# A decoder layer on one core: attention softmax in fewer VectorE instructions, three more chunks by seven products, six hand-overs reordered

## The chip, the core and the metric

The kernel runs on one core of a Trainium2 chip. The core has a matrix engine (TensorE, PE in the profile; PEld is its weight load), a vector engine (VectorE, DVE), a scalar engine that evaluates functions (ScalarE, ACT), a general one (GpSimd, POOL) and a queue engine that starts transfers (SyncE, SP). They run beside each other and wait for each other by semaphores. The metric is the device time of one execution in microseconds; less is better.

## The reference

One layer, 256 tokens of width 2048 in float32, batch 1. Two half-step SwiGLU blocks stand around a mixer of two branches:

```python
h = layer_norm(DN_ALPHA * h + 0.5 * swiglu(h, ffn1_w_in, ffn1_w_out), ln1_g, ln1_b)
q, k, v, qi, ki, wi, rx, rg, gates = split_cols(h @ w_in)
y_attn = dsa_attention(rope(q), rope(k), v, rope(qi), rope(ki), wi * c)   # 16 heads of 128, 4 key heads
y_rnn = rglru_branch(rx, rg, conv_w, conv_b, lru_wa, lru_ba, lru_wx, lru_bx, lru_lambda)
g_attn, g_rnn = split(sigmoid(gates), 2)
merged = g_attn * (y_attn @ w_attn_branch) + g_rnn * (y_rnn @ w_rnn_branch)
h = layer_norm(DN_ALPHA * h + merged @ w_out, ln2_g, ln2_b)
h = layer_norm(DN_ALPHA * h + 0.5 * swiglu(h, ffn2_w_in, ffn2_w_out), ln3_g, ln3_b)
```

The attention is sparse: an indexer scores every key for every query, the 64 best causal keys of a query are kept, and a head's softmax goes over these alone:

```python
_, idx = lax.top_k(score, topk)                     # topk = 64
s = where(valid, (q . k[idx]) * HEAD_DIM ** -0.5, -inf)
p = softmax(s);  o = p . v[idx]
```

## The kernel before, in words

**Numbers in two halves.** Matrices are multiplied in float32 precision from two reduced-precision halves: a weight piece `raw` becomes `wh` (a rounded copy, ACT, L243) and `wl` (the rest, DVE, L244), an activation tile becomes a high and a low half in the same way (for instance L860 on ACT and L861 on DVE, L803 and L804). A product is three matmuls: high by high, high by low, low by high (L674 to L676 over feature-major weights, L688 to L691 in pairs). Weights are streamed once: SP loads pieces of 128 x 1024, five of each half are kept, so L243 and L244 run a few pieces ahead of PE, and L243 of a piece waits until PE has finished with the `wh` five pieces before.

**Chunks by seven products.** Most products go by chunks of four 128 x 512 weight tiles. A plain chunk is 24 matmuls of 512 columns in two pieces. A chunk can also be computed with Strassen's seven products in Winograd's form: 42 matmuls of 256 columns in three and a half pieces (`blockF`, forms `p1q3`, `p2`, `q5p7` and the last). Its weights are sums that DVE makes first (L206, L210, L213), its activations are sums as well (`left`, L589 to L595, the tiles `sh` and `sl`), and at the end `joined` (L1178 to L1184) puts the block together from the products. `GATE_FAST` lists, for each of the eight blocks of 512 gate columns, which of the four chunks go this way.

**Order.** PE, SP and POOL run in the order in which the code is written. DVE and ACT are ordered by a scheduler ahead of time, with some work marked as of high priority. Small work between products is written as generators in lanes: at every new weight piece each lane makes one step (`on_piece`). So a step's distance in time is the length of a piece, 12 matmuls, of 512 columns or of 256.

**The heads.** In the middle of the gate blocks 0 to 5, sixteen heads pass through the lane `head`, four at a time (`head(h)`, L1247 on). The steps: scores on PE into PSUM (L1258, L1259; 128 + 256 columns for the two query tiles); scale and mask in one DVE pass (L1262) and the row maximum by two reductions (L1267); two exponentials with row sums on ACT (L1270); reciprocal of the sums and two products on DVE (L1272, L1274); three transposes on PE (L1278); the copy out on ACT (L1281); the product with the values (L1284, L1285). Before them the indexer makes the mask `bias` on DVE: the sum over 16 index heads (L1234), eight rounds of maximum and replace (L1239, L1240), and two closing steps (L1244, L1245). Between these, DVE runs a chain of small 128 x 20 instructions for the recurrent branch's constants (L516 to L567).

**The seams.** Where a layer norm stands between two products, PE cannot go on until the first tiles of the normed activation are there. `InnerNorm` does it for the first and second norm: `half(t)` norms the first two 512-wide blocks of token half t (L871), transposes them on PE (L852), scales and shifts them on ACT (L859, or L874 for later blocks), and splits them (L860, L861). Blocks 2 and 3 come by `Lazy`, which makes block number `k // 4 + 1 + ahead` when tile k is asked for; a block costs transposes (L885), scaling (L874) and splitting (L803, L804). Meanwhile `eager` runs the first eight k steps (L674 to L676, tiles `hs`). The last norm, `OuterNorm.finish`, computes the second token half at the end: statistics, the reciprocal root on POOL (L825, a power), products on DVE (L931, L935), a part on PE by a diagonal matrix `dg` (L946, L950), and the stores. Between the mixer and its output product the merged activation `mg` is split (L803, L804) and, for seven-product chunks, summed by `left_again`.

**The start.** SP loads the activation tiles `x` and the first weight pieces in turns.

Of the kernel before, what the change touches and what calls it, by code (L numbers as in the profile page):

```python
# [106 lines left out]
GATE_FAST = ((), (), (), (3,), FAST_A, FAST_A, (), ())  # L107
# [192 lines left out]
class Lazy:  # L300


    def __init__(self, n, per, make, ahead=1):
        self.n, self.per, self.make, self.ahead = n, per, make, ahead
        self.tiles = []
        self.made = 0
        self.halves = None
# [4 lines left out]
    def __getitem__(self, k):  # L312
        while self.made < min(self.n // self.per, k // self.per + 1 + self.ahead):
            self.tiles += self.make(self.made)
            self.made += 1
        return self.tiles[k]
# [3 lines left out]
def tile_layer(ctx, tc, x_fm, x_tm, pos, f1a, f1o, wA, wki, wB, wG, lru, wab, wrb, wo, f2a, f2o,  # L320
# [136 lines left out]
    W.load_to(3, load_x_fm)  # L457
    for k2 in range(4, NK // 2):
        load_x_fm(k2)
# [109 lines left out]
    with tc.manual_schedule():  # L569
        for k2 in range(4):  # L570
            xs += split_x(k2)
            W.split_to(k2, (256, 512, PIECE, PIECE)[k2])
        for k2 in range(4, NK // 2):
            xs += split_x(k2)
# [33 lines left out]
    def left_again(x, forms, chunks):  # L608

        for k in (2 * q + r for q in chunks for r in range(2)):  # L610
            f = [T1(), T1()]
            for c in range(2):
                V.tensor_tensor(f[c], x[2 * k + c][:, 0], x[2 * k + c][:, 1], op=OP.add)
            yield
            left(f, forms, k)
            yield
# [147 lines left out]
    def blockA(x, finish=None, lag=0, ln=None):  # L764

        ps = [MM(), MM()]
        n = len(x)

        def half(t, k, w):
            tokens(ps[t], x[k], t, w, k == 0, k == n - 1)

        k = 0
        if getattr(x, "halves", None):
            eager(x, ps)
            k = 8
        lead = 2 * lag
        ranges = [(k, k + 2) for k in range(k, n, 2)]
        if finish:  # L780
            ranges = ranges[:-lag] + [(n - lead, n)]
        for k0, k1 in ranges:
            ws = []
            for k in range(k0, k1):
                ws.append(W.unit(512))
                half(0, k, ws[-1])
            if finish and k1 == n:
                finish(ps)
            for k in range(k0, k1):
                if ln and k == n - 2:  # L790
                    ln.half(0)
                half(1, k, ws[k - k0])
        return ps
# [22 lines left out]
    class Norm:  # L816
        last = False

        def chain(self, t):
# [5 lines left out]
            G.tensor_tensor(r, ve, mhalf, op=OP.pow)  # L825
# [3 lines left out]
    class InnerNorm(Norm):  # L829


        def __init__(self, gk, bk, fast, after):
            self.gk, self.bk, self.fast, self.after = gk, bk, fast, after
            self.hs = Lazy(NK, 4, self.block, 2)
# [8 lines left out]
        def emit(self, t):  # L843
# [4 lines left out]
            for nb in range(2):  # L848
# [4 lines left out]
                for j in range(4):  # L853
# [5 lines left out]
                    A.activation(f, src, AF.Identity, scale=col(self.gk, k), bias=col(self.bk, k))  # L859
# [12 lines left out]

        def out(self, k, hl, f, src):
            A.activation(f, src, AF.Identity, scale=col(self.gk, k), bias=col(self.bk, k))  # L874
            split(hl, f)
# [25 lines left out]
    class OuterNorm(Norm):  # L901
# [7 lines left out]
        def load(self):  # L909


            for v in (self.g, self.b):
# [4 lines left out]
                self.rows.append([t[:, nb * 512:(nb + 1) * 512] for nb in range(4)])  # L917

# [332 lines left out]
    def head(h):  # L1251
# [10 lines left out]
        V.scalar_tensor_tensor(s, ps[:, :3 * P], ATT_SCALE, bias, op0=OP.mult, op1=OP.add)  # L1262
# [3 lines left out]
        for t in range(2):  # L1266
            V.tensor_reduce(nm[:, t:t + 1], part[t], axis=AX, op=OP.max, negate=True)  # L1267
        yield
        for t in range(2):
            A.activation(part[t], part[t], AF.Exp, bias=nm[:, t:t + 1], accum_out=sm[:, t:t + 1])  # L1270
        yield
        V.reciprocal(sm, sm)  # L1272
        for t in range(2):
            V.tensor_scalar(part[t], part[t], sm[:, t:t + 1], None, op0=OP.mult)  # L1274
# [230 lines left out]
    bg.add("left", left_again(mg, mg_forms, MG_FORMS))  # L1505
# [105 lines left out]
```

## Time and profile before

| | us |
|---|---|
| runs, median of 3 (lowest, highest) | 2243.09 (2242.83, 2244.89) |
| the profiled execution | 2242.38 |
| its span in the trace | 2240.6 |
| PE busy in the span | 2223.4 (99%), 14582 matmuls |
| DVE busy | 2101.5 (94%), 3019 instructions |
| ACT busy | 1434.7 (64%), 2008 instructions |

The profiled execution takes 1.8 us more than its span, before the first and after the last instruction; it lies 0.7 us under the median. A row of a timeline gives start, duration, engine, line, operation, output and inputs, shapes, count, and in brackets the idle time ahead of it with what ended it. A row of the waits gives who waited for whom, the total, the count and the longest. Line numbers are those of the kernel before. Matmuls overlap in the pipeline, so PE's pace is read from the distance of two starts and not from a row's duration.

### The profile page before, as it was taken

Reading aid. Unit: us, or ns where it says so; the run is one execution under the profiler, and the core shown is the slowest. Engines: PE = TensorE matmul, PEld = TensorE weight load, DVE = VectorE, ACT = ScalarE, POOL = GpSimd, SP = SyncE. Lnnn points to the kernel's source line nnn. Section 1 sums busy time; section 2 is a strip of 40 time slices with the busy share of each in tenths; the row PEclk is TensorE's granted clock in tenths of the full one; section 3 lists DMA queues with packets and bytes.
Section 4 is the critical chain, followed back from the end, with each engine's and each line's share of the span. In section 5 each row is a group of like instructions: output and inputs, shape, how many; then the busy total and the mean of one; then the engine's idle time right before and its main releaser. Section 6 shows DMA issues by size and latency. Waiting matters only on the chain.

```text
span 2240.6 us, 38639 instructions
## 1 busy us (share of the span) xinstructions
PE 2223.4 (99%) x14582; PEld 2056.5 (92%) x14582; DVE 2101.5 (94%) x3019; ACT 1434.7 (64%) x2008; POOL 125.5 (6%) x196
## 2 busy tenths in 40 slices
PE   9999999999999999999999999999999999999998
PEld 8999999999988898899999999988899999999997
DVE  8999999999988999899868879998999999999997
ACT  7666666666657655665567786555666666666663
POOL 0000000000000000001000002100000000000001
PEclk9999999999999999999999999999999999999999
DMA  9776766666675555648566658766677666676655
GB/s 344 232 232 218 244 216 217 236 223 237 221 250 188 179 197 172 209 137 306 194 192 195 197 188 317 273 212 205 219 239 228 232 227 233 228 241 213 221 200 188
DMA packets 126187, 498.62 MB, mean 223 GB/s; under 512 B 14608, under 2 KB 17424, under 8 KB 107312
## 3 DMA queue, kind: packets, MB, share of 16 engines
q1 hardware_dynamic: 107424, 451.98, 57.5%
q0 software_dynamic: 18576, 44.17, 8.5%
q8 instruction: 114, 1.87, 0.3%
q14 instruction: 73, 0.60, 0.1%
HBM read 464.63 MB, written 10.49 MB: 212 GB/s over the span
## 4 chain that ended last, share of the span: by engine, by line
PE 94%; DVE 3%; ACT 1%; issue 1%; DMA 1%; SPq 0%; POOL 0%; POOLq 0%; DVEq 0%; ACTq 0%
PE mm L688 20%; PE mm L689 20%; PE mm L691 20%; PE bp L689 6%; PE bp L691 6%; PE bp L688 6%; PE mm L1387 3%; PE mm L1388 3%; PE mm L1389 3%; DVE wl L244 1%; PE mm L674 1%; PE mm L676 1%; PE bp L1071 1%; PE mm L675 1%; ACT f L874 0%
## 5 line engine op out<-in xcount | busy, mean ns | idle before, releaser
L243 ACT ACTIVATE wh<-raw 128x1024 fp32r<-128x1024 f32 (+1 forms) x569 | 574.3, 1028 | 299.8 <-PE mm L689 170.7
L244 DVE TENSOR_TENSOR wl<-raw,wh 128x1024 fp32r<-128x1024 f32 (+1 forms) x569 | 662.6, 1185 | 82.2 <-ACT wh L243 81.5
L243 ACT ACTIVATE wh<-rf 128x1024 fp32r<-128x1024 f32 (+1 forms) x438 | 393.9, 914 | 199.0 <-PE mm L689 105.9
L244 DVE TENSOR_TENSOR wl<-rf,wh 128x1024 fp32r<-128x1024 f32 (+1 forms) x438 | 451.9, 1045 | 7.5 <-ACT wh L243 1.5
L688 PE MATMUL mm<-wh,hs 128*128 128x512 f32 (+1 forms) x872 | 297.3, 350 | 0.0
L689 PE MATMUL mm<-wh,hs 128*128 128x512 f32 (+1 forms) x872 | 292.1, 344 | 0.0
L688 PE MATMUL mm<-wh,g 128*128 128x512 f32 x656 | 249.3, 380 | 0.0
L689 PE MATMUL mm<-wh,g 128*128 128x512 f32 x656 | 248.6, 379 | 0.0
L243 ACT ACTIVATE wh<-ws 128x1024 fp32r<-128x1024 f32 x146 | 155.1, 1063 | 121.2 <-PE mm L689 72.1
L688 PE MATMUL bp<-wh,sh 128*128 128x256 f32 x876 | 213.7, 278 | 0.0
L689 PE MATMUL bp<-wh,sl 128*128 128x256 f32 x876 | 210.7, 275 | 0.0
L691 PE MATMUL mm<-wl,hs 128*128 128x512 f32 (+1 forms) x872 | 205.1, 344 | 0.0
L206 DVE TENSOR_TENSOR ws<-rf 128x1024 f32<-128x1024 f32 x146 | 178.5, 1223 | 5.0 <-DMA rf<-wab 1.6
L244 DVE TENSOR_TENSOR wl<-ws,wh 128x1024 fp32r<-128x1024 f32 x146 | 178.5, 1222 | 3.8 <-ACT wh L243 3.5
L688 PEld LDWEIGHTS mm<-wh,hs 128*128 128x128 f32 x872 | 165.8, 190 | 15.3 <-issue 1.3
L689 PEld LDWEIGHTS mm<-wh,hs 128*128 128x128 f32 x872 | 165.9, 190 | 13.6
L1387 PE MATMUL mm<-hs,wh 128*128 128x256 f32 x640 | 176.4, 276 | 0.0
L1389 PE MATMUL mm<-hs,wl 128*128 128x256 f32 x640 | 176.0, 275 | 0.0
L1388 PE MATMUL mm<-hs,wh 128*128 128x256 f32 x640 | 176.0, 275 | 0.0
L689 PEld LDWEIGHTS bp<-wh,sl 128*128 128x128 f32 x876 | 168.1, 192 | 1.2
L688 PEld LDWEIGHTS bp<-wh,sh 128*128 128x128 f32 x876 | 168.0, 192 | 1.2
L691 PE MATMUL mm<-wl,g 128*128 128x512 f32 x656 | 168.3, 379 | 0.0
(368 smaller groups left out, 4888.0 us busy)
## 6 DMA issues: line engine op xcount, KB each, us to landing
rf<-f1a SPq DMA_DIRECT2D x57, 1024.0 KB, 6.4
rf<-f2a SPq DMA_DIRECT2D x57, 1024.0 KB, 6.2
raw<-f1o SPq DMA_DIRECT2D x88, 512.0 KB, 7.8
raw<-f2o SPq DMA_DIRECT2D x88, 512.0 KB, 7.8
raw<-wB SPq DMA_DIRECT2D x80, 512.0 KB, 4.3
raw<-f2a SPq DMA_DIRECT2D x62, 512.0 KB, 4.0
raw<-f1a SPq DMA_DIRECT2D x61, 512.0 KB, 4.0
raw<-wG SPq DMA_DIRECT2D x54, 512.0 KB, 4.0
```

Source lines behind the costliest of these rows:

```text
L206: v.tensor_tensor(t, b[:, 0:4:3], b[:, 1:2].to_broadcast([P, 2, 4, P]), op=OP.add)
L243: nc.scalar.activation(hp, src, AF.Copy)
L244: self.last = nc.vector.tensor_tensor(lp, src, hp, op=OP.subtract)
L674: T.matmul(ps, xh, w[0], start=start, stop=False)
L675: T.matmul(ps, xh, w[1], start=False, stop=False)
L676: T.matmul(ps, xl, w[0], start=False, stop=stop)
L688: T.matmul(ps, xh, w[0], start=start, stop=False)
L689: T.matmul(ps, xl, w[0], start=False, stop=False)
L691: T.matmul(ps, xh, w[1], start=False, stop=stop)
L1387: T.matmul(ps, w[0], xh, start=first, stop=False)
L1388: T.matmul(ps, w[0], xl, start=False, stop=False)
L1389: T.matmul(ps, w[1], xh, start=False, stop=last)
```

## The change

1. `GATE_FAST`: chunk 3 of blocks 1 and 2 and chunk 2 of block 3 go by seven products as well.
2. The head softmax: L1262 and L1267 become one DVE instruction per query tile, straight from PSUM, which adds the mask to the scores, multiplies by the negative scale and gives the row minimum of the result; each is followed by a short read of that minimum (`ISA` rows in the order). The exponential takes scale -1. The two products by the reciprocal (L1274) become two scaled copies on ACT.
3. `InnerNorm`: of the scalings, every second one of the second token half and every odd tile of blocks 2 and 3 are done by DVE instead of ACT; a later block is made two tiles later; after the first FFN the transposes of the first token half stand one k step (three matmuls) later.
4. `left_again` for `mg` starts four steps later and makes two steps into one.
5. The last norm's second half takes a root on ACT and a reciprocal on DVE in place of POOL's power; a dummy root is issued earlier.
6. At the start, only two x and weight pairs are loaded ahead; the rest is issued behind a one-column DVE copy of the first split tile.

```diff
-GATE_FAST = ((), (), (), (3,), FAST_A, FAST_A, (), ())
+GATE_FAST = ((), (3,), (3,), FAST_A, FAST_A, FAST_A, (), ())
...
-        while self.made < min(self.n // self.per, k // self.per + 1 + self.ahead):
+        while self.made < min(self.n // self.per, (k + self.early) // self.per + 1 + self.ahead):
...
-    W.load_to(3, load_x_fm)
-    for k2 in range(4, NK // 2):
-        load_x_fm(k2)
+    W.load_to(1, load_x_fm)
...
             xs += split_x(k2)
+            if k2 == 0:
+                V.tensor_copy(xraw[2][:, :1], xs[0][:, 1, :1])
+                W.load_to(3, load_x_fm)
+                for j in range(4, NK // 2):
+                    load_x_fm(j)
...
-    def left_again(x, forms, chunks):
+    def left_again(x, forms, chunks, lag=0):
+        for _ in range(lag):
+            yield
...
-            yield
+            if not lag:
+                yield
             left(f, forms, k)
...
-                if ln and k == n - 2:
+                if ln and k == n - (1 if n == 8 else 2):
                     ln.half(0)
...
-            G.tensor_tensor(r, ve, mhalf, op=OP.pow)
+            if self.last and t == 1:
+                A.activation(r, ve, AF.Sqrt)
+                V.reciprocal(r, r)
+            else:
+                G.tensor_tensor(r, ve, mhalf, op=OP.pow)
...
-            self.hs = Lazy(NK, 4, self.block, 2)
+            self.hs = Lazy(NK, 4, self.block, 1, 2)
...
-                    A.activation(f, src, AF.Identity, scale=col(self.gk, k), bias=col(self.bk, k))
+                    self.scaled(f, src, k, t == 1 and j % 2)
...
+        def scaled(self, f, src, k, by_v):
+            if by_v:
+                V.tensor_scalar(f, src, col(self.gk, k), col(self.bk, k), op0=OP.mult, op1=OP.add)
+            else:
+                A.activation(f, src, AF.Identity, scale=col(self.gk, k), bias=col(self.bk, k))
         def out(self, k, hl, f, src):
-            A.activation(f, src, AF.Identity, scale=col(self.gk, k), bias=col(self.bk, k))
+            self.scaled(f, src, k, k % 2)
...
+            A.activation(SM(1), stats["st"][1][:, 6:7], AF.Sqrt)
...
-        V.scalar_tensor_tensor(s, ps[:, :3 * P], ATT_SCALE, bias, op0=OP.mult, op1=OP.add)
...
-            V.tensor_reduce(nm[:, t:t + 1], part[t], axis=AX, op=OP.max, negate=True)
+            a, b = t * P, (1 + 2 * t) * P
+            V.tensor_tensor_reduce(s[:, a:b], ps[:, a:b], bias[:, a:b], -ATT_SCALE, -2 * NEG, OP.add, OP.min,
+                                   nm[:, t:t + 1])
...
-            A.activation(part[t], part[t], AF.Exp, bias=nm[:, t:t + 1], accum_out=sm[:, t:t + 1])
+            A.activation(part[t], part[t], AF.Exp, scale=-1.0, bias=nm[:, t:t + 1], accum_out=sm[:, t:t + 1])
...
-            V.tensor_scalar(part[t], part[t], sm[:, t:t + 1], None, op0=OP.mult)
+            A.activation(part[t], part[t], AF.Copy, scale=sm[:, t:t + 1])
...
-    bg.add("left", left_again(mg, mg_forms, MG_FORMS))
+    bg.add("left", left_again(mg, mg_forms, MG_FORMS, LAG_MG[1] + 1))
```

Where the change moves rows: first ACT at the seam after the first FFN, at the upper half of the sixth tile for token half 1 (`hs_7434` before, `hs_7438` in the change; `f` and the `hs` beside it belong to block 2). A row names the line, the operation, the tiles with their numbers (output first) and the shape. Before:

```order
L803 ACTIVATE hs_7600<-f_7595 128x256
L860 ACTIVATE hs_7433<-t_7552 128x128
L859 ACTIVATE t_7556<-bp_7547,cols 128x128
L874 ACTIVATE f_7631<-bp_7626,cols 128x256 x2
L803 ACTIVATE hs_7632<-f_7631 128x256
L803 ACTIVATE hs_7636<-f_7631 128x256
L874 ACTIVATE f_7645<-bp_7640,cols 128x256 x2
L803 ACTIVATE hs_7646<-f_7645 128x256
L803 ACTIVATE hs_7650<-f_7645 128x256
L860 ACTIVATE hs_7434<-t_7556 128x128
```

And in the change (its L870 is L860 before, L887 the scaling, L809 is L803):

```order
L870 ACTIVATE hs_7435<-t_7539 128x128
L887 ACTIVATE t_7553<-bp_7548,cols 128x128
L870 ACTIVATE hs_7436<-t_7543 128x128
L870 ACTIVATE hs_7437<-t_7553 128x128
L870 ACTIVATE hs_7438<-t_7557 128x128
L887 ACTIVATE t_7561<-bp_7548,cols 128x128
L243 ACTIVATE wh_7581<-raw_7330 128x1024
L887 ACTIVATE f_7592<-bp_7587,cols 128x256
L870 ACTIVATE hs_7439<-t_7561 128x128
L809 ACTIVATE hs_7593<-f_7592 128x256
```

The copies of the first eight tiles now stand ahead of the later blocks' work, half of the scalings are gone from ACT, and weight splits stand in between.

Second, DVE where the mask is finished and the first heads begin (`bias` is the mask, `bp` the scores in PSUM). Before:

```order
L1245 TENSOR_TENSOR bias<-bias,tri 128x128
L560 TENSOR_TENSOR s_9965<-s_9965,s_9894 128x20
L561 TENSOR_SCALAR s_9965<-s_9965 128x20
L560 TENSOR_TENSOR s_9965<-s_9965,s_9894 128x20
L561 TENSOR_SCALAR s_9965<-s_9965 128x20
L244 TENSOR_TENSOR wl_9914<-raw_9734,wh_9913 128x1024
```

and after eight more small rows and two more L244 the first L1262. In the change:

```order
L206 TENSOR_TENSOR ws_10030<-rf_9856 128x1024
L244 TENSOR_TENSOR wl_9913<-raw_9731,wh_9912 128x1024
L244 TENSOR_TENSOR wl_9932<-rf_9532,wh_9931 128x1024
L1261 TENSOR_SCALAR bias<-bias 128x256
L558 TENSOR_TENSOR s_9958<-s_9958,s_9895 128x20
L210 TENSOR_TENSOR rf_9856<-ws_10030,rf_9856 128x4x128
L244 TENSOR_TENSOR wl_9955<-raw_9785,wh_9954 128x1024
L1262 TENSOR_TENSOR bias<-bias,tri 128x128
L1284 ISA s_9994,s_9995<-bp_9964,bias 128x128
L1284 ISA s_9995 128x1
```

The closing step of the mask (L1245, now L1262) has come to stand behind the splits and sums of the added chunks, directly ahead of the new passes of four heads; the rest of the small chain went behind these.

Third, ACT at the same four heads, in the change (L1288 the exponentials, L1292 the scaled copies that replace L1274 of DVE):

```order
L1288 ACTIVATE s_10009,s_10011<-s_10009,s_10010 128x128
L1288 ACTIVATE s_10009,s_10011<-s_10009,s_10010 128x256
L243 ACTIVATE wh_10056<-raw_9882 128x1024
L1292 ACTIVATE s_9994<-s_9994,s_9996 128x128
L1292 ACTIVATE s_9994<-s_9994,s_9996 128x256
L1292 ACTIVATE s_9999<-s_9999,s_10001 128x128
L1292 ACTIVATE s_9999<-s_9999,s_10001 128x256
```

All eight copies stand behind the last exponential and a weight split. On PE, four pieces stand between the four heads' scores and their transposes before and now: 48 matmuls of 512 columns before, 24 of 512 and 24 of 256 in the change, and the scores themselves stand one plain piece earlier.

More of the change, by code (lines that the diff above doesn't have):

```diff
@@ L300, with __init__ @@
 class Lazy:
-    def __init__(self, n, per, make, ahead=1):
-        self.n, self.per, self.make, self.ahead = n, per, make, ahead
+    def __init__(self, n, per, make, ahead=1, early=0):
+        self.n, self.per, self.make, self.ahead, self.early = n, per, make, ahead, early
         self.tiles = []
```

## The prediction

> **What bounds the kernel now.** I read the page first, then PE's waits, then each wait's place in the timelines of PE, ACT and DVE. The page's busy times and its chain:
>
> ```profile
> PE 2223.4 (99%) x14582; PEld 2056.5 (92%) x14582; DVE 2101.5 (94%) x3019; ACT 1434.7 (64%) x2008; POOL 125.5 (6%) x196
> PE 94%; DVE 3%; ACT 1%; issue 1%; DMA 1%; SPq 0%; POOL 0%; POOLq 0%; DVEq 0%; ACTq 0%
> ```
>
> PE sets the end, so a change pays by fewer matmul columns or by fewer waits of PE. Who waited for whom, PE's rows (us in total, times, longest):
>
> ```profile
> PE mm L674 <- ACT hs L860: 5.2, 2, 2.6
> PE mm L688 <- ACT wh L243: 1.4, 2, 1.2
> PE bp L950 <- ACT dg L946: 1.3, 1, 1.3
> PE bp L1278 <- ACT pT L1281: 0.7, 1, 0.7
> PE mm L689 <- DVE mg L804: 0.7, 1, 0.7
> PE bp L852 <- DVE y L871: 0.6, 1, 0.6
> ```
>
> All of PE's waits together are some 10 us: no edit of waits can be worth more. But DVE is close behind PE, and just ahead of the heads it has nothing left (window; busy of PE, PEld, DVE, ACT, POOL; clock; DMA):
>
> ```profile
> 840.00:860.00 20.00, 20.00 (x134) 18.21 (x134) 19.94 (x41) 13.18 (x17) 0.00 (x0) 1.00 0.45 136
> 880.00:900.00 20.00, 20.00 (x100) 17.65 (x100) 19.68 (x65) 8.29 (x10) 1.08 (x2) 1.00 0.64 199
> 920.00:940.00 20.00, 20.00 (x109) 17.88 (x108) 14.64 (x32) 12.73 (x29) 1.07 (x2) 1.00 0.55 171
> ```
>
> **Gate chunks.** PE's pace is the distance of two starts, of 512 columns and of 256:
>
> ```profile
> 906.31 0.38 PE L688 MATMUL mm<-wh,hs 128*128 128x512 f32 x1
> 906.53 0.38 PE L689 MATMUL mm<-wh,hs 128*128 128x512 f32 x1
> 976.47 0.28 PE L688 MATMUL mm<-wh,hs 128*128 128x256 f32 x1
> 976.58 0.28 PE L689 MATMUL mm<-wh,hs 128*128 128x256 f32 x1
> ```
>
> 0.2155 us (averaged over a run of them) and 0.112. A plain chunk is 24 x 0.2155 = 5.17 us, one by seven products 42 x 0.112 = 4.70, so three chunks give **-1.4 us** on PE. DVE pays, by these rows (the first two are groups of the page, with count, busy time and mean ns):
>
> ```profile
> L243 ACT ACTIVATE wh<-raw 128x1024 fp32r<-128x1024 f32 (+1 forms) x569 | 574.3, 1028 | 299.8 <-PE mm L689 170.7
> L206 DVE TENSOR_TENSOR ws<-rf 128x1024 f32<-128x1024 f32 x146 | 178.5, 1223 | 5.0 <-DMA rf<-wab 1.6
> 847.04 0.70 DVE L210 TENSOR_TENSOR rf<-ws,rf 128x512 f32<-128x512 f32 x1
> 859.41 0.42 DVE L1181 TENSOR_TENSOR stg<-bp,stg 128x256 f32<-128x256 f32 x1
> 860.08 1.27 DVE L1184 TENSOR_TENSOR stg<-stg,mm 128x512 f32<-128x512 f32 x2
> ```
>
> On DVE the next instruction starts about 0.09 before a row's end. A chunk adds one L206 (1.13), L210 and L213 (0.6 each) and one and a half L244 (1.14 each, by the row of two below), 4.1 us; two blocks newly need `joined` (four of 0.33, two of 0.6), 2.5 us each: 17 us for DVE in all.
>
> **Head softmax.** The first four heads before, DVE and then ACT:
>
> ```profile
> 892.30 0.29 DVE L1245 TENSOR_TENSOR bias<-bias,tri 128x128 f32<-128x128 f32 x1
> 895.24 0.18 DVE L563 TENSOR_TENSOR s<-s,s 128x20 f32<-128x20 f32 x1
> 895.45 0.18 DVE L564 SCALAR_TENSOR_TENSOR s<-s,s 128x20 f32<-128x20 f32 x1
> 895.83 2.35 DVE L244 TENSOR_TENSOR wl<-raw,wh 128x1024 fp32r<-128x1024 f32 x2
> 898.10 1.02 DVE L1262 SCALAR_TENSOR_TENSOR s<-bp,bias 128x384 f32<-128x384 f32 x2
> 899.03 1.12 DVE L1267 TENSOR_REDUCE s<-s 128x1 f32<-128x128 f32 x4
> 907.64 0.55 DVE L1274 TENSOR_SCALAR s<-s,s 128x128 f32<-128x128 f32 x2
> 904.19 0.49 ACT L1270 ACTIVATE s<-s,s 128x256 f32<-128x256 f32 x1
> 905.07 0.49 ACT L1270 ACTIVATE s<-s,s 128x256 f32<-128x256 f32 x1
> ```
>
> By starts, a head costs DVE 0.47 + 0.52 + 0.46 = 1.45 us, beside a reciprocal that stays. The new pass is in no row. Below it cannot be cheaper than L1262's stream, 0.47, and above it has no reason to exceed mask and maximum together, 0.99; it reads the same columns once, in two instructions with a short read behind each, so I take 0.73 (two fixed parts and two reads more than L1262). That is 0.7 saved per head, 11 us for 16, bounds 7 to 15. So DVE ends with some 6 us more in 840 to 1010 us; the free 5 us in 920 to 940 alone hold that, later. ACT gets two copies per head, 0.3 and 0.4, 11 us into 35% free time. The sums of load cost PE nothing. What costs is **where** it falls, next.
>
> **The stall at the first four heads.** A head moves on one step per weight piece, and a piece by seven products lasts half as long. PE before:
>
> ```profile
> 898.35 0.57 PE L688 MATMUL mm<-wh,hs 128*128 128x512 f32 x1
> 908.90 1.47 PE L1278 MATMUL bp<-ident,s 128*128 128x128 f32 x12
> 910.13 0.46 PE L688 MATMUL mm<-wh,hs 128*128 128x512 f32 x1
> ```
>
> Four plain pieces lie between scores and transposes, 48 x 0.2155 = 10.3 us; DVE's last division ends at 908.19, 0.7 us ahead. In the change's order these are two plain and two fast pieces, 2 x 2.59 + 2 x 1.34 = 7.9 us, the scores stand one plain piece (2.6) earlier, and 0.5 was saved before: PE wants the transposes 5.6 us earlier, at 903.3 on this clock, and would leave them at 904.5. But DVE does not get earlier. From a common piece of weights to the first softmax instruction its list now has two L206, two L210, one L213 more (4.1 us) and a half L244 less (-0.5), while 13 small L56x instructions (-2.2, 0.17 each) went behind: the first pass starts 1.3 us later, at 899.4. From there: four heads 2.9; those 13 small ones, now ahead of the reciprocals, 0.21 each by the two rows at 895, 2.7; two L244 2.3; L213 0.6; four reciprocals, as small as L563, 0.6; the last two copies on ACT 0.7. That is 9.8, so the last head is ready at 909.2, PE's last transpose is through 0.4 later, and PE resumes near 909.6 instead of 904.5. ACT alone, from 899.8 (four pairs of exponentials by 0.88, from 904.19 to 905.07, three L243 by 1.0, four pairs of copies by 0.7), would be done at 909.2 too. The **stall is 5.1 us**. DVE restarts after the norm ahead of it about 1 us earlier against PE than before, which takes 1 off; a pass at the dear bound adds 1. I take **+5.0**, bounds 2 and 7. Later heads keep 7.0 us or more between scores and transposes, as before, where the tightest cost the one wait of 0.7: +-0.5, taken as 0.
>
> **The two inner-norm seams.** PE and ACT at the first:
>
> ```profile
> 686.21 0.44 PE L676 MATMUL mm<-wh,hs 128*128 128x512 f32 x1
> 689.25 0.48 PE L674 MATMUL mm<-wh,hs 128*128 128x512 f32 x1 [2.61 <-ACT hs L860]
> 682.26 1.02 ACT L874 ACTIVATE f<-bp,cols 128x256 f32<-128x256 f32 x2
> 683.16 0.74 ACT L803 ACTIVATE hs<-f 128x256 fp32r<-128x256 f32 x2
> 688.84 0.36 ACT L860 ACTIVATE hs<-t 128x128 fp32r<-128x128 f32 x1
> ```
>
> PE wants the sixth tile's upper half, and that L860 stands behind eight L874 and eight L803 of the blocks after it, 682.26 to 688.84. The start after 686.21 is 3.04 later where 0.2155 was due: 2.83 lost. In the change that copy stands ahead of all of them, and half of the scalings are DVE's (4 x 0.2 + 4 x 0.33 = 2.1 us there, 2.7 less on ACT). With eight instructions ahead of it and itself at no more than 0.36 each, from 679.7 where ACT's timeline has the second half's first scaling, it is done by 683. So the 2.83 goes, and a like 0.15 behind it. The earlier wait (L852, 0.6) is removed by moving the transposes three matmuls on, but most of that returns, since the low parts L861 then stand behind L813, L814 and L871 on DVE: I count 0.1. **-3.1** (-3.9 to -2.0). The second seam has the same wait of 2.6 and keeps its transposes' place: **-2.9** (-3.1 to -1.8).
>
> **Merge seam.** L804's four low parts now stand ahead of the sums for the seven-product operands on DVE, so the wait of 0.7 there goes: **-0.7** (-0.9 to +0.5, as the held-back sums can be late in their turn).
>
> **Start.** PE's 1.4 for L243 lie in the first 20 us, where L243 itself waits for loads. Holding back later x and weight loads behind a DVE copy makes the first pieces land sooner and the fifth later, and the bytes stay the same, so a wait moves rather than goes: **0** (-0.7 to +1).
>
> **Tail.**
>
> ```profile
> 2232.10 1.41 DVE L931 SCALAR_TENSOR_TENSOR y<-y,s,row 128x512 f32<-128x512 f32 x2
> 2235.53 0.88 DVE L935 SCALAR_TENSOR_TENSOR y<-y,s,row 128x256 f32<-128x256 f32 x2
> ```
>
> POOL's power, for which `dg` and with it L950 wait, becomes a root on ACT, which has no weights left to split there, and a reciprocal on DVE. But DVE is the later one: it is busy without a gap from 2232.10 to 2236.4 and its last product feeds the last store, so an earlier `dg` frees nothing, and the reciprocal costs **+0.15** (-0.3 to +0.3).
>
> **Sum** against the profiled execution (2242.38 us, span 2240.6): -1.4 - 3.1 - 2.9 - 0.7 + 0.15 + 5.0 = -2.95, so 2239.4; the median of the runs is 0.7 above that execution: **2240.1**, I say 2240. Without the stall it would be -7.95.
>
> **Rivals.** (a) *The heads don't stall*: DVE's order as listed is kept, but it gets there 4 us sooner, because it leaves the norm's seam earlier than I allow. For it: seam work of DVE is interleaved now. Against: it is never idle for long from 700 to 900. 2234 to 2238.5. (b) *PE comes back slow.* The trace shows a slow PE once, at its start:
>
> ```profile
> 1.92 3.27 PE L439 MATMUL bp<-wu 128*128 128x512 f32 x7 [1.92 <-DVE wu L436]
> ```
>
> 0.47 us per matmul, against 0.2155 later. After the 2.6 us wait at 689 it is back at pace at once. Seven matmuls so slow would add 7 x 0.25 = 1.8 to a stall longer than any here: 2241.9. [...] (c) *DVE gives the seams back.* From the first seam to 860 us DVE is at 19.9 of 20 us, and PE arriving 3 us earlier may wait for L244 instead: +3 on the forecast, 2243. (d) *Slower*: the additional step from DVE back to ACT stalls PE at every later head, too. From -2.95, twelve heads at 0.25 us each make it even, at 0.63 each 0.2% slower; one whole L243 (1.06) ahead of each copy would be +12.7, 2253. Against it: only one wait of 0.7 stands there now, with 7.0 us in hand.
>
> **Chances.** Forecast with stall at full clock, 2238 to 2242: 0.41; (a) 0.36; (b) 0.09; (c) 0.08; (d) 0.06. Range 2234 to 2243.5: it holds (a) and (b) but for their edges, half of (c), not (d). What this kernel's measurement can tell from no change is about 0.2%, 4.5 us. Faster by more, under 2238.6: (a) and 0.04 of the forecast, 0.40. Slower by more: (d) and an edge of (c), 0.07. Within: 0.53.
>
> **What would show it.** Right: in PE's waits the rows of L674 are gone or under 0.5, and one new row of 4 to 5 us, transposes (L1296) for ACT's copies (L1292), near 900 us; the new DVE pass under 0.5 us per instruction; matmuls fewer columns by 1.4 us. Wrong: no wait at the first heads (then (a)), waits of PE for L244 after the seams (c), matmuls at 0.43 behind the stall (b), or a wait for L1292 at most heads (d).

## The result and the profile after

The changed kernel takes 2257.7 us (median of 4 runs, 2256.52 to 2259.24), the kernel before 2243.45 beside it: a ratio of 1.0060, 95% interval 1.0048 to 1.0072, 14 us slower. The forecast was 2240, with 2234 to 2243.5 as its range. Later runs were on other chips, where the kernel before took 2244.8 to 2245.6, so each kernel is read by its ratio to the kernel before on the same chip.

The page of the changed kernel answers the first lines quoted in the prediction. Then the rows of PE's waits that matter here; the line numbers are the new ones: L694 to L697 are the matmuls L688 to L691, L1275 and L1276 the scores, L1284 the new DVE pass, L1288 the exponentials, L1292 the copies that divide, L1296 the transposes, L1302 and L1303 the product with the values, L1196 to L1201 `joined`, L862 and L881 the norm's transposes and subtraction.

```profile
PE 2228.1 (99%) x14636; PEld 2060.8 (91%) x14636; DVE 2111.5 (94%) x3048; ACT 1447.1 (64%) x2035; POOL 125.0 (6%) x195
```

```profile
PE bp L1275 <- DVE s L1284: 4.7, 1, 4.7
PE bp L1296 <- DVE stg L1196: 4.2, 2, 2.5
PE mm L694 <- ACT wh L243: 2.3, 3, 1.4
PE mm L694 <- DVE z L1076: 1.8, 1, 1.8
PE bp L862 <- DVE y L881: 1.7, 1, 1.7
PE bp L1275 <- DVE stg L1196: 1.3, 1, 1.3
PE bp L1296 <- ACT s L1292: 0.3, 1, 0.3
```

L674's 5.2 us, which the seams were to remove, are gone. In their place stand waits of a kind that the kernel before has nowhere: scores and transposes (`bp`) that wait for the pass that reads other scores, or for the recombination of a gate block (`stg`). They have no operand in common with it. What they share is the PSUM pool `bp`, which has four buffers (`bufs=4`, as `mm` has four): a chunk by seven products accumulates four of its seven products in two of them, each held from its first matmul until `joined` has read it.

Where the time went is read from the starts (first column) of the same six instructions on PE. In the timeline of the kernel before:

```profile
44.02 0.60 PE L1071 MATMUL bp<-ident,z 128*128 128x128 f32 x4
...
714.37 0.60 PE L1158 MATMUL bp<-ident,stg 128*128 128x128 f32 x4
...
1091.36 0.28 PE L1387 MATMUL mm<-hs,wh 128*128 128x256 f32 x1
...
1556.37 1.06 PE L852 MATMUL bp<-ident,y 128*128 128x128 f32 x8
...
1600.89 0.60 PE L1071 MATMUL bp<-ident,z 128*128 128x128 f32 x4
...
1642.99 0.60 PE L1071 MATMUL bp<-ident,z 128*128 128x128 f32 x4
```

The same six in the changed kernel:

```profile
45.23 0.60 PE L1088 MATMUL bp<-ident,z 128*128 128x128 f32 x4
...
712.41 0.60 PE L1175 MATMUL bp<-ident,stg 128*128 128x128 f32 x4
...
1105.75 0.28 PE L1405 MATMUL mm<-hs,wh 128*128 128x256 f32 x1
...
1571.74 1.07 PE L862 MATMUL bp<-ident,y 128*128 128x128 f32 x8 [1.67 <-DVE y L881]
...
1612.91 0.60 PE L1088 MATMUL bp<-ident,z 128*128 128x128 f32 x4
...
1657.20 0.60 PE L1088 MATMUL bp<-ident,z 128*128 128x128 f32 x4
```

| stretch | change minus before at its end | in the stretch |
|---|---|---|
| start, to 44 | +1.2 | +1.2 |
| first FFN and norm, to 714 | -2.0 | -3.2 |
| projections, gates, heads, to 1091 | +14.4 | +16.4 |
| branches and merge, to 1556 | +15.4 | +1.0 |
| second norm, to 1601 | +12.0 | -3.4 |
| behind it, to 1643 | +14.2 | +2.2 |
| to the end of the span | +14.0 | -0.2 |

The whole loss lies in the heads. The three chunks save their 1.4 us of matmuls in the same stretch, so 17.8 us were lost there. PE's waits between 890 and 985 add up to 12.1 us, where the kernel before has 0.7. The changed kernel's first group of heads, PE's rows:

```profile
892.32 0.60 PE L1276 MATMUL bp<-hT,hT 128*128 128x256 f32 x2
897.60 0.80 PE L1275 MATMUL bp<-hT,hT 128*128 128x128 f32 x2 [4.69 <-DVE s L1284]
898.69 0.99 PE L694 MATMUL mm<-wh,hs 128*128 128x512 f32 x1
899.47 0.63 PE L695 MATMUL mm<-wh,hs 128*128 128x512 f32 x1
899.90 0.63 PE L694 MATMUL mm<-wh,hs 128*128 128x512 f32 x1
...
904.94 0.38 PE L694 MATMUL mm<-wh,hs 128*128 128x512 f32 x1
905.16 0.38 PE L695 MATMUL mm<-wh,hs 128*128 128x512 f32 x1
...
913.40 1.54 PE L1296 MATMUL bp<-ident,s 128*128 128x128 f32 x6 [2.52 <-DVE stg L1196]
```

Three heads' scores find a buffer: one of the four is held by the block's first sum (its matmuls began at 883.6, the second sum's stand at 903.6). The fourth waits 4.7 us, until the pass has read the first ones. And behind the wait two starts lie 0.43 us apart where 0.2155 is PE's pace: PE came back at half speed, until about 903. The same after 913. The trace holds the granted clock, too (windows as in the prediction; PE's clock is the third number from the end):

```profile
897.60:903.00 5.40, 5.40 (x14) 4.40 (x15) 3.83 (x25) 0.38 (x3) 0.00 (x0) 0.50 0.33 97
913.40:916.60 3.20, 3.20 (x11) 2.84 (x12) 1.16 (x3) 0.98 (x2) 0.00 (x0) 0.50 0.75 314
```

5.4 and 3.2 us at half clock lose 2.7 and 1.6 us, so 4.3 of the 17.8. ACT and DVE show how the stall spreads:

```profile
897.24 0.40 ACT L1288 ACTIVATE s<-s,s 128x128 f32<-128x128 f32 x1 [4.76 <-DVE s L1284]
902.75 1.06 ACT L243 ACTIVATE wh<-raw 128x1024 fp32r<-128x1024 f32 x1 [5.02 <-issue]
908.90 2.86 ACT L1292 ACTIVATE s<-s,s 128x128 f32<-128x128 f32 x8
911.67 0.62 ACT L243 ACTIVATE wh<-rf 128x512 fp32r<-128x512 f32 x1
896.91 0.28 DVE L1284 CUSTOM_DVE_ANT_0 s<-bp,bias 128x128 f32<-128x128 f32 x1
897.12 0.42 DVE L1284 CUSTOM_DVE_ANT_0 s<-bp,bias 128x256 f32<-128x256 f32 x1
897.47 0.28 DVE L1284 CUSTOM_DVE_ANT_0 s<-bp,bias 128x128 f32<-128x128 f32 x1
912.32 0.69 DVE L244 TENSOR_TENSOR wl<-rf,wh 128x512 fp32r<-128x512 f32 x1 [2.06 <-ACT wh L243]
912.93 0.41 DVE L1196 TENSOR_TENSOR stg<-stg,bp 128x256 f32<-128x256 f32 x1
```

After one exponential ACT comes to a weight split whose buffer PE has not given back, since PE stands at the scores; it waits 5.0 us, and the seven other exponentials wait behind it. (The profile names no releaser for this wait. Without PE's stall, in the run below with the sums in other buffers, the same split starts at 897.66 with no wait.) Then come the eight copies, a split behind them, DVE's L244 behind that split, and L1196 behind L244: only that frees the buffer that the third head's transposes need.

### The profile page after: what moved, and what is told of

It reads as the page before. It is cut to its first block, busy times and chain, and to the rows that moved or that the text cites. A ratio compares the mean times of both kernels' runs of the same rounds, so it can differ in the third digit from the quotient of the medians.

```text
span 2254.6 us, 38791 instructions
## 1 busy us (share of the span) xinstructions
PE 2228.1 (99%) x14636; PEld 2060.8 (91%) x14636; DVE 2111.5 (94%) x3048; ACT 1447.1 (64%) x2035; POOL 125.0 (6%) x195
## 3 DMA queue, kind: packets, MB, share of 16 engines
q8 instruction: 114, 1.87, 0.3%
## 5 line engine op out<-in xcount | busy, mean ns | idle before, releaser
L243 ACT ACTIVATE wh<-raw 128x1024 fp32r<-128x1024 f32 (+1 forms) x563 | 568.4, 1027 | 281.8 <-PE mm L695 163.1
L244 DVE TENSOR_TENSOR wl<-raw,wh 128x1024 fp32r<-128x1024 f32 (+1 forms) x563 | 655.0, 1183 | 83.2 <-ACT wh L243 80.4
L243 ACT ACTIVATE wh<-rf 128x1024 fp32r<-128x1024 f32 (+1 forms) x447 | 401.8, 915 | 194.1 <-PE mm L695 103.9
L244 DVE TENSOR_TENSOR wl<-rf,wh 128x1024 fp32r<-128x1024 f32 (+1 forms) x447 | 460.3, 1042 | 11.1 <-ACT wh L243 5.0
L694 PE MATMUL mm<-wh,hs 128*128 128x512 f32 (+1 forms) x860 | 292.9, 350 | 0.0
L695 PE MATMUL mm<-wh,hs 128*128 128x512 f32 (+1 forms) x860 | 287.5, 344 | 0.0
L694 PE MATMUL mm<-wh,g 128*128 128x512 f32 x656 | 249.5, 380 | 1.8 <-DVE z L1076 1.8
L694 PE MATMUL bp<-wh,sh 128*128 128x256 f32 x894 | 217.9, 278 | 0.0
L697 PE MATMUL mm<-wl,hs 128*128 128x512 f32 (+1 forms) x860 | 201.5, 342 | 0.0
L244 DVE TENSOR_TENSOR wl<-ws,wh 128x1024 fp32r<-128x1024 f32 x149 | 181.7, 1220 | 5.1 <-ACT wh L243 3.0
L694 PEld LDWEIGHTS mm<-wh,hs 128*128 128x128 f32 x860 | 164.6, 191 | 15.0 <-issue 1.3
L694 PEld LDWEIGHTS bp<-wh,sh 128*128 128x128 f32 x894 | 171.4, 192 | 1.2
L697 PE MATMUL mm<-wl,g 128*128 128x512 f32 x656 | 168.3, 379 | 0.0
```

The costliest lines, as they stand in the source:

```text
L243: nc.scalar.activation(hp, src, AF.Copy)
L244: self.last = nc.vector.tensor_tensor(lp, src, hp, op=OP.subtract)
L694: T.matmul(ps, xh, w[0], start=start, stop=False)
L695: T.matmul(ps, xl, w[0], start=False, stop=False)
L697: T.matmul(ps, xh, w[1], start=False, stop=stop)
```

## The experiments

Three theories were put up. **A, accumulators:** a chunk by seven products takes two of the four `bp` buffers from the heads. **B, late mask** (the forecast's): the mask and the first pass come late on DVE, and the division's step to ACT lengthens the way to the transposes. **C, load:** DVE has too much to do. Later **D, slow clock:** after some waits PE runs at half pace, as behind the 4.7 us wait above (0.43 us per matmul, granted clock 0.50).

### The gates put back

```diff
-GATE_FAST = ((), (3,), (3,), FAST_A, FAST_A, FAST_A, (), ())
+GATE_FAST = ((), (), (), (3,), FAST_A, FAST_A, (), ())
```

> The changed kernel with GATE_FAST as it was before: no chunk of gate blocks 1 and 2 by seven products, one of block 3. Theory A (accumulators): a chunk by seven products holds two of the four `bp` buffers of PSUM from its first product to its recombination, so that the heads' scores and transposes find none; then nearly all of the 17 us of waits between 890 and 985 us go and 1.4 us of matmuls come back: 2241 to 2243. Theory B (the forecast's: mask late, division handed to ACT): the handing over to ACT is still there, so 3 to 5 us of waits for L1292 or L1284 stay at the first heads: 2245 to 2247. Theory C (sum of DVE's load): the load falls by 17 us, waits shrink in proportion, 2244 to 2250.

2238.82 us against 2245.48: ratio 0.9969 (0.9957 to 0.9980). No wait at the heads is left among PE's waits, though the pass and the copies are those of the change. The mask, however, is early again: its closing step starts at 890.77, with the chunks' sums gone from ahead of it, so this run does not part A from a late mask. A alone had a number like this, and was still 2 us short. The rest of the change is worth 7 us, the three chunks cost 20 by the two ratios, 16.5 by the two profiled spans (2238.1 and 2254.6).

### The gates alone

The kernel before, with the opposite edit.

> The kernel before with only GATE_FAST of the change. Theory A: the same waits for `bp` buffers, at scores, transposes and recombination, 12 to 18 us, less 1.4 of matmuls: 2254 to 2260. Theory B: the division is on DVE again, only the later mask costs: 2 to 4 us, 2244 to 2246. Theory C: DVE carries more here than in the change (old softmax and new chunks), so at least the loss of the change: over 2258.

2263.04 us: ratio 1.0079 (1.0064 to 1.0094), 18 us slower, 3 more than A said. Its trace has a stretch of 3.4 us at half clock behind each of the two old seam waits, 1.7 us lost each, which A's number left out. Its waits at the heads (old numbers: L1258 the scores, L1262 the old pass, L1278 the transposes, L1179 `joined`):

```profile
PE bp L1258 <- DVE s L1262: 4.6, 1, 4.6
PE bp L1278 <- DVE stg L1179: 4.5, 2, 2.7
PE bp L1258 <- DVE stg L1179: 1.4, 1, 1.4
```

These are the change's waits nearly to the tenth, with the old softmax. So neither the new pass nor the division on ACT makes them. Of B only the late mask is left as a rival here, since the chunks put it late in this run, too.

### The softmax alone

```diff
-        V.scalar_tensor_tensor(s, ps[:, :3 * P], ATT_SCALE, bias, op0=OP.mult, op1=OP.add)
...
+            V.tensor_tensor_reduce(s[:, a:b], ps[:, a:b], bias[:, a:b], -ATT_SCALE, -2 * NEG, OP.add, OP.min,
+                                   nm[:, t:t + 1])
...
-            V.tensor_scalar(part[t], part[t], sm[:, t:t + 1], None, op0=OP.mult)
+            A.activation(part[t], part[t], AF.Copy, scale=sm[:, t:t + 1])
```

> The kernel before with only the head softmax of the change. Theory A: no buffer is held longer, PE was not waiting here: 2242.5 to 2244, no wait over 1 us at the heads. Theory B: one more handing over per group, 2 to 5 us of waits for L1292: 2245 to 2248.

2245.24 us, ratio 0.9997 (0.9988 to 1.0007): nothing, as A and the forecast's sum had it. DVE's saved time bought nothing here, where PE did not wait for it. Its trace had something else. The same seam wait as in the kernel before, 2.61 us for L860, and then:

```profile
689.48 0.69 PE L674 MATMUL mm<-wh,hs 128*128 128x512 f32 x1 [2.61 <-ACT hs L860]
689.97 0.63 PE L675 MATMUL mm<-wl,hs 128*128 128x512 f32 x1
690.39 0.63 PE L676 MATMUL mm<-wh,hs 128*128 128x512 f32 x1
...
692.95 0.42 PE L676 MATMUL mm<-wh,hs 128*128 128x512 f32 x1
693.21 0.38 PE L674 MATMUL mm<-wh,hs 128*128 128x512 f32 x1
693.42 0.38 PE L675 MATMUL mm<-wl,hs 128*128 128x512 f32 x1
```

Some eight matmuls at 0.425, 1.7 us lost, at both seams of this trace (granted clock 0.50 from 689.7 to 693.0) and of the one before it, and at neither seam of the trace that the forecast was made from.

### The seams alone

The kernel before with `Lazy`'s `early`, `scaled`, and the first half's transposes one step later.

> The kernel before with only the inner-norm edits (scalings on DVE, later blocks made two tiles later, first transposes one step later). The forecast: -3.1 and -2.9, 2237.5. By the trace of the changed kernel: -3.2 at the first seam, -3.35 at the second, and 2 us given back some 80 us behind the second: 2238.5 to 2240. If DVE's extra work is what gives back, the wait behind the second seam is there without any other edit.

2238.37 us, ratio 0.9972 (0.9960 to 0.9984): 6.3 us by the ratio, 7.1 by the medians. By the same six instructions its trace gains 3.0 and 3.4 us at the two seams and gives 1.4 back behind the second; it ends 4.7 us before the trace of the kernel before, both at full clock. The rest fits the half clock that goes with the waits: the record of each execution has a mean granted clock of 1.000 for five of these six, and of 0.997 to 0.999 for all 18 of the kernel before on that chip. The wait behind the second seam (L1065 is L1059 before) stands without any other edit, and DVE has no free time ahead of it (windows as in the prediction):

```profile
PE mm L688 <- DVE z L1065: 1.0, 1, 1.0
1600.00:1620.00 20.00, 20.00 (x125) 18.37 (x124) 20.00 (x28) 12.62 (x20) 0.00 (x0) 1.00 0.52 170
1620.00:1640.00 20.00, 18.99 (x121) 17.16 (x121) 20.00 (x25) 12.37 (x17) 1.80 (x2) 1.00 0.89 274
```

### Block 1 plain, and block 3 alone

```diff
+GATE_FAST = ((), (), (3,), FAST_A, FAST_A, FAST_A, (), ())
```

> The changed kernel with gate block 1 plain again; blocks 2 and 3 keep their added chunks. The first four heads start within block 1. Theory A (accumulators): no buffer of sums is held there, so the waits of the first group (scores for the pass, transposes for the recombination, the slow matmuls behind each, 11 to 12 us between 890 and 917) go and the later ones (5 us between 940 and 985) stay: 4 us above the kernel before instead of 14, 0.5 of it the chunk's lost saving. Theory B (late mask): the mask is earlier by one chunk's work, 4 us, and the waits go with it just as well, but ACT's copies still cost 2 to 3 us: 5 to 7 above.

2249.46 us against 2245.57, ratio 1.0013 (1.0004 to 1.0022): 3 us above the kernel before instead of 13.5. Block 1's chunk costs 10 us by the ratios. Not all of the first group's wait went with it: 1.8 us for L1292 were left at its transposes (909.29), which is B's share, and 0.9 behind them, where block 2's first sum waits for a `bp` buffer until ACT has copied a transpose out (L1299). A like wait of 2.2 for L1299 stands at the last heads' transposes (981.55).

```diff
+GATE_FAST = ((), (), (), FAST_A, FAST_A, FAST_A, (), ())
```

> The changed kernel with only the third added chunk (gate block 3); blocks 1 and 2 plain. Theory A (accumulators): block 3 held two buffers before, for its chunk 3; with chunk 2 too it holds them for half the block, in which the last heads go: 0 to 3 us of waits near 975, the slow clock behind them in some runs; 2239 to 2242 where the version without any added chunk has 2238.8. Theory B (late mask) has nothing at this place: 2238.3, half a microsecond less than that version.

2248.59 us against 2244.78, ratio 1.0016 (1.0006 to 1.0025). From 0.9969 without added chunks this single one costs 10 us, three times what I gave it at most. It puts `joined` of its block into the heads (L1302 waited 2.3 us for L1196, at 968), and PE's granted clock was 0.50 from 969.2 to 975.9. Blocks 2 and 3 together cost no more than block 3 alone.

### The sums in other buffers

The same instructions on every engine as in the change, and PE's in the same order, but the two buffers of sums of blocks 1 and 2 come from `mm`:

```diff
-                e = [BP(), BP()]
+                e = [(acc or BP)() for _ in range(2)]
...
-        s, own = product(hs, gate_forms, GATE_FAST[b])
+        s, own = product(hs, gate_forms, GATE_FAST[b], MM if b in (1, 2) else None)
```

> The changed kernel, with the two buffers of sums of gate blocks 1 and 2 taken from the four `mm` buffers instead of the four `bp` ones; nothing else. This separates buffers from lateness: order and load are the same. Theory A: PE no longer waits for scores (L1275 for L1284) or at transposes for L1196; what is left at the first heads is the late mask, 3 to 6 us at the transposes, and blocks 2 and 3 may wait at their first product until the recombination has read `mm`, 1 to 3 us each: 5 to 10 us above the kernel before instead of 14. Theory B: the waits move to other instructions, but their sum stays, 13 to 15 above.

2249.04 us, ratio 1.0018 (1.0009 to 1.0028): 9.4 of the 13.5 us come back (1.0060 to 1.0018) with nothing but the pool of two buffers edited; that leaves 4 us above the kernel before, where A had said 5 to 10. The scheduler moved a few instructions of DVE and ACT with it (one weight split stands two exponentials earlier at the first heads), but up to the first heads' pass DVE's order is the same, and the pass starts at 896.93 where the change has 896.91. The scores' wait for L1284 is gone and the first group's transposes wait for the copies. Two of its rows, the second from the last heads, where block 3's sums still lie in `bp`:

```profile
PE bp L1296 <- ACT s L1292: 3.1, 1, 3.1
PE bp L1296 <- DVE stg L1196: 1.6, 1, 1.6
```

That settles A against C, since DVE's and ACT's work was not touched, and against the late mask as the main cause, since the mask is as late as in the change. The first row is the wait that the forecast had named, laid bare: 3.1 us, with another 1.6 for the transposes (2.81 us to the next product, 1.23 in the kernel before) and 1.5 for matmuls at half pace behind it.

The same for block 3, once with its chunk alone (`MM if b == 3`), once with all three (`MM if b in (1, 2, 3)`):

> The run with the third added chunk alone, with one thing different: gate block 3 keeps its sums in two `mm` buffers instead of two `bp` ones. That run waited at the last heads for the recombination (L1302 and L1275 for L1196) and lost 4.5 us with the slow matmuls behind it, another 6 us by 1090. Theory A (accumulators): those waits go, 8 to 10 us less, 6 to 8 us under the kernel before. A wait of 1 to 2 us where the next block's first product needs `mm` is possible. If buffers are not it, 3 to 4 us above the kernel before, as that run.

2244.18 us against 2244.94, ratio 0.9999 (0.9990 to 1.0009). Here PE, DVE and ACT have the same instructions in the same order as in the run with block 3's chunk alone, so the pool by itself makes the difference.

> The changed kernel with the sums of gate blocks 1, 2 and 3 in `mm` buffers. With those of 1 and 2 there it stood 4 us above the kernel before, with waits of 0.9, 0.7, 0.5 and 1.8 at the last heads and 3.3 plus the slow clock at the first. Theory A: the last heads' waits go too, 3 to 4 us, some of the slow clock with them: within 1 us of the kernel before. What is left against the version without added chunks is the late mask alone, 5 to 7 us at the first heads: so both causes together give the change's loss.

2250.68 us, ratio 1.0023 (1.0012 to 1.0033). With block 3's chunk alone the move returns 4 of the 10 us, half of what I expected, and with all three it returns nothing beyond the run with two, where I expected to be within 1 us of the kernel before. The waits at the heads' buffers are gone in both, but new ones stand at the next block's first product, for the same `joined`. First the run with block 3 alone, then the one with all three:

```profile
PE mm L694 <- DVE stg L1199: 1.8, 1, 1.8
PE mm L694 <- DVE stg L1196: 1.0, 1, 1.0
```

```profile
PE bp L1296 <- ACT s L1292: 3.1, 1, 3.1
PE mm L694 <- DVE stg L1199: 2.0, 1, 2.0
PE mm L694 <- DVE stg L1196: 1.6, 1, 1.6
```

So it is not the pool `bp` alone. A block by seven products holds two `mm` buffers besides its two of sums; with the sums there as well it holds all four until DVE has recombined it, and the next block's first product waits. A block that held four of the eight buffers made someone wait here, whichever pool they came from: 2.3 us at L1302 with block 3's sums in `bp`, 2.8 at L694 with them in `mm`. In the last trace the three rows (6.7 us) and three stretches at half clock (906 to 909, 974 to 981, 1650 to 1653; some 6 us lost) make up most of the 12 us that the ratios put between this run and the version without added chunks.

### Without the start's edit, and without the merge's

The changed kernel with gates and start as before:

```diff
...
-    W.load_to(1, load_x_fm)
+    W.load_to(3, load_x_fm)
+    for k2 in range(4, NK // 2):
+        load_x_fm(k2)
...
```

> The changed kernel with the gate blocks and the start as before. By the landmarks of the traces the start's reordering costs 1.0 to 1.4 us, so this is that much under the version with the gates alone put back, which was 6.7 under the kernel before: 7.5 to 8.5 under it. If the start is neutral, as forecast, 6.5 to 7.

And in addition:

```diff
-    bg.add("left", left_again(mg, mg_forms, MG_FORMS, LAG_MG[1] + 1))
+    bg.add("left", left_again(mg, mg_forms, MG_FORMS))
```

> As the one before, and the sums for the merged activation not held back either. The forecast's merge term was -0.7, so this should be 0.7 slower than the one before. By the traces the wait of 0.9 at the merge went, but 0.5 came back 50 us later at a weight split and 1.3 to 1.6 at the first transposes of the second norm: then this is 0.8 to 1.2 faster than the one before, 8.5 to 9.5 under the kernel before.

2238.54 and 2236.97 us against 2245.57: ratios 0.9969 (0.9957 to 0.9981) and 0.9965 (0.9953 to 0.9977). The times do not separate them from each other or from the version with only the gates put back. At the first of the six instructions above, all seven traced kernels with the new start are late against the one before, by 1.1 to 1.7 us, and all six others with the old start by 0.0 to 0.5; so the start's edit costs about a microsecond. For the merge the trace of the first of the two runs has no wait of 0.7 at the merge, but one of 0.3 at the second norm, and the second has the 0.7: no difference that a run here resolves. The last version is the fastest of all by its median, 7.9 us under the kernel before by the ratio.

### PE kept busy in the seam's wait

The kernel before with ten matmuls, whose result nobody reads, where PE waits for L860:

```diff
         for k in range(8):
+            if k == 5:
+                idle = MM().rearrange("p (q h) -> p q h", h=2)
+                for _ in range(10):
+                    T.matmul(idle, halves_of(x[4], 1)[0], ws[4][0], start=True, stop=True)
             tokens(ps[1], x[k], 1, ws[k], k == 0, False)
```

> The kernel before, with ten matmuls of 512 columns, whose result nobody reads, put where PE waits 2.6 us at each inner-norm seam (2.2 us of work in 2.6 of wait; everything else keeps its order). It separates the wait from what follows it. Theory D (slow clock after a wait): in some executions PE runs 8 matmuls at 0.427 instead of 0.2155 us after such a wait, 1.7 us at each seam, which the trace of the kernel before did not catch and those with the gates alone and the softmax alone did; with PE kept busy no trace shows it, the waits of 2.6 shrink to 0.3 or 0.4, and the median falls by 1 to 3.4 us against the kernel before on the same chip, to its lowest runs, with a narrower spread. If the slow matmuls have another cause, or are rare, the median stays within 0.5 us.

2243.37 us (2241.73 to 2245.23) against 2244.78 (2242.31 to 2247.18), ratio 0.9995 (0.9986 to 1.0004). Its one trace has waits of 0.9 in all in place of 5.2, and no matmul at half pace behind them. The median falls by 1.4 us, within what D allows, but the interval holds 1: the gain is not settled by this run. The clock is. The record has a mean granted clock for each execution: 1.000 in all 11 with the ten matmuls, and 1.000 in only 3 of 21 of the kernel before on the same chip, 0.997 to 0.999 in the others. Those 3 have a median of 2242.42 us, the 13 at 0.998 one of 2245.25. So most executions of the kernel before pay for the half clock, some 3 us by this comparison and 3.4 by two stretches of 1.7. Why the filled version, at full clock throughout, still spreads from 2241.7 to 2245.2 is open.

## Why the prediction was wrong, step by step

**The step that failed** is in the part on the head softmax and the stall: "The sums of load cost PE nothing. What costs is where it falls", with the later heads "+-0.5, taken as 0". That load costs nothing held. But I counted instructions and their places on DVE and ACT, and of the added chunks only their work, not the buffers they hold: the sum has no term for them. Two of the four `bp` buffers, through a stretch in which the heads need one buffer each for scores, transposes and output, cost 9.4 us by the run that moved the sums of blocks 1 and 2, and 3.8 by the one that moved block 3's alone. The later heads, taken as 0, have waits of 4.6 us in the change (945 to 984) against 0.7 before. And 4.3 us were lost to the half clock behind such waits. The code quoted for the kernel and the rows `bp<-wh,sh` of the profile before both show which pool the sums lie in; the seven-product blocks before overlap the last heads only, and the 0.7 us of L1278 there was a first sign.

**The stall at the first four heads**, +5.0 with bounds 2 and 7, was right in mechanism and in size, though only the run with the sums of blocks 1 and 2 in `mm` shows it. The changed kernel's first pass starts at 896.91, which is 898.9 on the clock before (it runs 2.0 early at 714), where I had worked out 899.4 less up to 1. With the sums out of the way, PE comes to the transposes at 901.3 (903.3 on the clock before, as worked out), waits 3.1 us and takes 1.6 longer for them: 4.7. The half clock behind it, 1.5, belongs to rival (b). In the change the stall is buried under the other waits, and its row has 0.3.

**The new pass** was taken at 0.73 us per head. By starts it takes 0.56 (896.91 to 897.47): the short read of the first half starts at 897.12, with the second half's pass, and adds nothing. That was worth nothing, as the run with the softmax alone shows.

**Rival (b), the slow clock,** came true, behind waits that I had not forecast and at more than my price (1.8): 2.7 us behind the 4.7 us wait, with eight to nine matmuls at 0.43, twice 0.2155, and 1.6 behind the wait at 913. No row of the kernel before shows that 0.43, which the forecast names; its one slow stretch, at the start, has 0.47. And what I had read beside it, "After the 2.6 us wait at 689 it is back at pace at once", was one execution's luck: in the trace of the softmax alone the same wait of 2.61 us has eight matmuls at 0.425 behind it. A wait of 1.87 at 1635, in the run without gates, start and merge, had some six slow matmuls behind it, too; that execution's mean granted clock is 0.999.

**The seams** were right: -3.2 and -3.4 in the trace, for -3.1 and -2.9 forecast. Of the second one's, 2.2 us came back 40 us later, by the mechanism of rival (c): PE arrives earlier and waits for a DVE that has no free time. I had priced that rival at +3 and given it 0.08.

**The chunks'** -1.4 stands in the matmul count (54 more of them, each short) and is measured by no run by itself; **the tail's** +0.15 is not measured by itself either: the whole stretch behind 1643 came out at -0.3 to +0.7 against the kernel before in the nine traces that have the new tail. **The start's** 0 was +1.2, just over its bound, and **the merge's** -0.7 was not there in the sum: the wait went, but 1.7 us stand at the second norm's first transposes (L862). Why these are late there is open: the version that differs only in the start has 0.3 instead of 1.4 at that place, 1500 us later, and no run here tells why.

**Rival (d)**, slower, named the later heads but the wrong cause: the copies on ACT, which cost nothing that the run with the softmax alone resolves.

## What to carry to other kernels

Count buffers like an engine: for each added piece of work write down which pool it takes from, from which instruction to which, and who else draws on that pool in that stretch. A wait between two instructions that share no operand was such a shortage here, and handing the softmax's work from DVE to ACT did not cure it (4.7 us with the new softmax, 4.6 with the old). And where PE stood at a wait for a buffer (4.7 us), the engines behind it carried it on: PE held back ACT's weight split by 5.0 us, that the exponentials, those DVE, and DVE the buffer, for which PE then stood another 2.5 us.

## What the runs showed of the hardware that was not expected

PE's half pace after a wait did not go by the wait's length alone. The same wait of 2.61 us, with the same instructions around it, was followed by 0.2155 us per matmul in the execution that the forecast was made from, and by 0.425 for eight matmuls in the trace of the softmax alone. The 4.7 us wait of the changed kernel was followed by nine matmuls at 0.43, and a wait of 1.87 in the run without gates, start and merge by some six at half pace. In the changed kernel's trace the granted clock was 0.50 from 896.2 to 903.0 and from 913.3 to 916.7: 6.8 and 3.4 us. Ten matmuls whose result nobody reads, put into the waits of 2.61, went with a mean granted clock of 1.000 in 11 of 11 executions, against 3 of 21 without them. So one trace without slow matmuls behind a wait is no evidence that the next execution has none, and what a removed wait gives can be more than its length: behind the wait of 2.61 another 1.7 us were lost.
